# Waiting tasks that sleep, wider pacing, and a sixth pair in seven products, in a GLA + NSA + SwiGLU layer

## The chip, the core and the metric

One core of one Trainium2 chip runs the whole layer in one launch. The metric is the device time of an execution in microseconds; of several executions the median is given. A profiled execution is timed too; its trace covers a span a little shorter than its time.

## What is computed

A decoder layer on 256 tokens of width 2048, all in float32: two attention groups, gated linear attention (GLA, 4 heads) and native sparse attention (NSA, 8 query heads over 2 key heads), read one normalised input through one projection; their outputs go through one output projection; a SwiGLU feed-forward block (FFN) of width 5632 follows.

```python
n = rms_norm(x, attn_norm_g)
g_qkv, g_lr, g_out, nq, kc, vc, ks, vs, kw, vw, ng = split(n @ w_in)
q, k, v = split(silu(causal_short_conv(g_qkv, gla_conv_w)))       # width 4
gla = rms_norm(chunked_gla(q, k, v, log_sigmoid(g_lr @ w2 + b) / 16), norm_g) * silu(g_out)
nsa = g0 * attend(q, compress(kc, vc)) + g1 * attend(q, selected(ks, vs)) + g2 * attend(q, window(kw, vw))
h = x + concat(gla, nsa) @ w_out
m = rms_norm(h, ffn_norm_g)
out = h + (silu(m @ w_gate) * (m @ w_up)) @ w_down
```

## The kernel before

**Split numbers.** Every weight block and activation is split into a rounded part hi (a copy on ScalarE, ACT) and a rest lo (a subtraction on VectorE, DVE): lines 137 and 138 for `w_in` and `w_out`, 641 and 642 in the FFN. A product is then three matmuls (hi x hi, hi x lo, lo x hi). A main matmul is 128x128 by 128x512; there are 2,592 at line 283 (projections and the FFN's down part), 1,896 at line 1147 (gate and up) and 90 at line 1288.

**Main work and side work.** A projection `proj(c0, evac)` of 512 columns is 96 main matmuls and ends in evictions (L478 for the GLA blocks and kc/vc). The projections run in the order: gate and low-rank columns, q, k, v in two blocks, kc/vc, ks/vs, kw/vw, nq in two blocks; then `w_out` in two halves; then the FFN's blocks. What the mixers do between them is written as generators and put into `urgent` or `later`: `conv` (the short convolution, with `turn_pair` for the transposes at L210 and STT steps at L492, then `to_qk` or `to_v` with the Silu at L502 or L510), `gla_decay` (exp at L545 and L547, DVE at L551 to L558, products at L584), `gla_turn`, `compress` (Silu at L794, product at L803), `turn_kc`, `key_turn`, `turn_q`, and `nsa_mix` (L930 and L941 belong to its compressed branch).

`drive(mains, pace)` draws main matmuls; each is worth 2 units, and for every `pace` units it calls `side()` once. `side()` goes on with the first task of `urgent`, or of `later` if there is none. A task that must give other engines time yields: each bare `yield` uses up one call of `side()`, with nothing done, while all tasks behind it stand still. A third queue, `background`, is called once every `rate` units: `sum_rows` loads FFN weights (SP queue), adds them on DVE (L1079) and stores the sums through the POOL queue (L1083).

**What sets the order.** The order in which the program issues work comes from these calls, then from a scheduler and from the pools' buffers (4 hi and 4 lo, 8 PSUM banks). Each engine then works through its own list in order: an instruction at the head that waits holds up all behind it on that engine. On ACT an ACT_TABLE_LOAD stands wherever exp follows Silu or Silu follows exp.

**Pairs in the FFN.** Gate and up of one block of 512 columns take eight pairs of weight blocks. A pair is either plain (24 main matmuls) or done in seven products (21 main matmuls), for which sums of the weight rows are needed: made beforehand by `sum_rows` for the pairs in `SUMS`, or on the spot by DVE (L1178, L1179, L1180). Block 1 has the order 0, 1, 2, 6, 3, 4, 5, 7, the set (0, 2, 3, 4, 5) in seven products, and prepared sums for 2, 3, 4, 5.

Of the kernel before, what the change touches and what calls it, by code (L numbers as in the profile page):

```python
# [17 lines left out]
NT = S // P  # L18
# [19 lines left out]
def kernel(  # L38
# [43 lines left out]

    def side():

        for queue in (urgent, later):
            while queue:
                try:
                    next(queue[0])
                    return
                except StopIteration:  # L90
                    queue.pop(0)
# [123 lines left out]

    cols = kp.tile([P, 164], F32, name="cols")
# [8 lines left out]
    def cols_rest():  # L225
        for _ in range(8):
            yield
        nc.gpsimd.memset(w2b, 0.0)
        with behind(last["dma"]):
            small_loads()  # L230
        for _ in range(20):
            yield
        pc = bank()
        transpose(pc[:, 0:P], rows2)
        transpose(pc[:, P:P + 20], rows[:20, :], 20)
        nc.vector.tensor_copy(cols[:, 36:164], pc[:, 0:P])
        nc.vector.tensor_copy(cols[:, 16:36], pc[:, P:P + 20])
        TS(kgain, gains[:, 1:4], gains[:, 0:1], None, ALU.mult)

# [241 lines left out]
    def conv(u, ct, dst):  # L481

        for _ in range(8):
            yield
        for pair in range(2):
            ps = yield from turn_pair(u, pair)
            y = g2([2, S])
            for c in range(2):
                ch = ct + 2 * pair + c
                act(y[:, c, :], ps[:, c, :], AF.Copy, scale=cw[:, 3, ch:ch + 1])  # L490
                for i in range(1, 4):
                    STT(y[:, c, i:], ps[:, c, :S - i], cw[:, 3 - i, ch:ch + 1], y[:, c, i:], ALU.mult, ALU.add)  # L492
            yield from dst(pair, y)
# [6 lines left out]
    def to_qk(near, far):  # L500
        def f(pair, y):
            act(near[:, pair, 0 if near is kk else 1], y[:, :, 0:P], AF.Silu)  # L502
            act(far[:, pair, 0 if far is qq else 1], y[:, :, S - 1:P - 1:-1], AF.Silu)
            yield
        return f

    def to_v(b):
        def f(pair, y):
# [4 lines left out]
            for _ in range(10):  # L513
                yield
# [12 lines left out]
    GAP0, GAP1 = 8, 4  # L527
# [100 lines left out]
    def gla_turn(h, y):  # L628
        for _ in range(20):
            yield  # L630
        if h % 2 == 0:
            m_h[h // 2], m_l[h // 2] = g4([4, S], F32R), g4([4, S], F32R)
        p = bank()
        for j in range(2):
            for t in range(NT):
                transpose(p[:, j * S + t * P:j * S + (t + 1) * P], y[:, t, j * P:(j + 1) * P])
            yield
        put_mix(h // 2, slice(2 * (h % 2), 2 * (h % 2) + 2), slice(0, S), p.rearrange("p (j s) -> p j s", j=2))

# [7 lines left out]
    def gla_mix():  # L647
        res = [{} for _ in range(4)]
        yield from gla_decay(0, GAP0)
# [28 lines left out]
    def turn_kc(u):  # L678
        for _ in range(8):
            yield  # L680
# [44 lines left out]
    def key_turn(br, t, kk):  # L725
        for _ in range(15):
            yield
# [7 lines left out]
        STT(kl, pv, g, f32(kh), ALU.mult, ALU.subtract)  # L735

# [14 lines left out]
    def compress():  # L751
# [13 lines left out]
        for w in range(2):  # L765
# [21 lines left out]
            for _ in range(6):  # L787
                yield
# [10 lines left out]
            for _ in range(9):  # L799
# [48 lines left out]
    def turn_q(kv, q):  # L848
        for _ in range(18):
            yield  # L850
# [99 lines left out]
    def nsa_mix():  # L950
# [3 lines left out]
        def ready(u):  # L954
            while u[0] not in nq:
# [17 lines left out]
    def w_out_half(half):  # L973
        for n in range(4):
# [21 lines left out]
    PAIRS7, FIRST7 = tuple(range(8)), {0: (0, 2, 4), 1: (0, 2, 3, 4, 5)}  # L996
# [278 lines left out]
    def down_last():  # L1275
# [68 lines left out]
        for t, bk in enumerate((banks[4], at[1])):  # L1344
# [12 lines left out]
    rate[0] = 18  # L1357
    drive([proj(C_KC, ev_kc), proj(C_KS, ev_kv(0)),
           proj(C_KW, ev_kv(1), ((0, 256), (256, 280))), proj(C_NQ, ev_nq(0))], 2.5)
    later.append(nsa_mix())  # L1360
    drive([proj(C_NQ + 512, ev_nq(1))], 2.5)
    rate[0] = 14
    drive([w_out_half(0)], 2)
# [46 lines left out]
```

## Time and profile before

| | us |
|---|---|
| median of 3 runs | 1107.42 (1107.02 to 1109.54) |
| the profiled execution's own time | 1108.26 |
| its span in the trace | 1106.5 |
| PE busy, of the span | 1096.7 |
| DVE busy | 992.7 |
| ACT busy | 751.5 |

The stages lie roughly so in the trace: input projections and mixers to 385 us, the second half of `w_out` to 417 us, FFN block 0 and block 1's gate and up from there to about 500 us, then seven-product blocks alternating with down parts of 96 matmuls to the end. PE rows of a trace are pipelined: a matmul's row is 0.39 us long while the next one starts 0.23 us after it. A note in brackets gives how long an engine sat idle before the row, and what it waited for.

### The profile page before, as it was taken

The numbers are of one execution on the slowest core, as the hardware profiler recorded it, in microseconds if no ns is written. First come the engines' busy times: TensorE is split into PE (matmuls) and PEld (weight loads), VectorE is DVE, ScalarE is ACT, GpSimd is POOL, SyncE is SP. The second block draws the span as 40 slices with busy tenths as digits, with TensorE's granted clock in tenths as the row PEclk, the third lists the DMA queues.
The fourth block names the chain that finished last, engine by engine and source line by source line (L and its number), as shares of the span: only waits on it lengthen the run. The fifth ranks groups of instructions, "written<-read, shape, count | busy, mean of one in ns | idle before, by whom it ended". The sixth has DMA issues, their size and how long they took to land.

```text
span 1106.5 us, 14596 instructions
## 1 busy us (share of the span) xinstructions
PE 1096.7 (99%) x5290; PEld 900.4 (81%) x5290; DVE 992.7 (90%) x1277; ACT 751.5 (68%) x1017; POOL 71.7 (6%) x134
## 2 busy tenths in 40 slices
PE   9999999999999999999999999999999999999998
PEld 8888788897777787888888788888888888888886
DVE  6678887879689788997999999999999999999997
ACT  6646867554566596667586776768586866768684
POOL 4110000123200000000000000000000000000000
PEclk9999999999999999999999999999999999999999
DMA  7999677579765646785565657566665657577763
GB/s 271 340 332 346 210 256 243 196 274 375 282 239 192 236 154 218 242 307 200 192 219 202 217 185 256 195 234 215 216 227 201 214 198 252 182 252 234 237 229 114
DMA packets 124850, 259.61 MB, mean 235 GB/s; under 512 B 6709, under 2 KB 8793, under 8 KB 124778
## 3 DMA queue, kind: packets, MB, share of 16 engines
q1 hardware_dynamic: 113514, 219.86, 58.1%
q0 software_dynamic: 10368, 37.75, 9.2%
q10 hardware_dynamic: 896, 1.07, 0.3%
q8 instruction: 41, 0.67, 0.3%
q14 instruction: 31, 0.25, 0.1%
HBM read 239.78 MB, written 18.87 MB: 234 GB/s over the span
## 4 chain that ended last, share of the span: by engine, by line
PE 88%; DVE 5%; DMA 3%; ACT 3%; issue 1%; POOL 0%; ACTq 0%; DVEq 0%
PE bank L283 44%; PE bank L1147 36%; PE bank L210 3%; DMA raw<-in_w_in_dram 2%; PE bank L1288 2%; DVE ftwo L642 2%; DVE lo L138 1%; PE bank L584 1%; PE bank L946 1%; PE bank L873 1%; ACT hi L137 1%; DMA fraw<-in_w_down_dram 1%; ACT ftwo L641 0%; PE bank L779 0%; DVE g L1178 0%
## 5 line engine op out<-in xcount | busy, mean ns | idle before, releaser
L1147 PE MATMUL bank<-ftwo,g 128*128 128x512 f32 x1848 | 431.6, 392 | 0.2 <-ACT ftwo L641 0.2
L1147 PEld LDWEIGHTS bank<-ftwo,g 128*128 128x128 f32 x1848 | 342.4, 188 | 76.6 <-DVE ftwo L642 3.3
L283 PE MATMUL bank<-hi,g 128*128 128x512 f32 (+1 forms) x1088 | 321.5, 375 | 0.3 <-ACT hi L137 0.2
L642 DVE TENSOR_TENSOR ftwo<-fraw,ftwo 128x1536 fp32r<-128x1536 f32 (+1 forms) x130 | 257.9, 1984 | 8.8 <-ACT ftwo L641 7.5
L641 ACT ACTIVATE ftwo<-fraw 128x1536 fp32r<-128x1536 f32 (+1 forms) x130 | 216.9, 1670 | 32.9 <-DMA fraw<-in_w_up_dram 23.2
L283 PE MATMUL bank<-ftwo,g 128*128 128x512 f32 x960 | 221.4, 391 | 0.4 <-ACT bank L1259 0.4
L283 PEld LDWEIGHTS bank<-hi,g 128*128 128x128 f32 x1088 | 192.4, 188 | 31.7 <-issue 0.8
L283 PEld LDWEIGHTS bank<-ftwo,g 128*128 128x128 f32 x960 | 179.2, 188 | 39.9 <-ACT bank L1259 2.6
L137 ACT ACTIVATE hi<-raw 128x1024 fp32r<-128x1024 f32 (+3 forms) x124 | 130.6, 1057 | 95.8 <-PE bank L283 73.2
L283 PE MATMUL bank<-lo,g 128*128 128x512 f32 (+3 forms) x544 | 193.6, 375 | 0.9 <-DVE lo L138 0.6
L138 DVE TENSOR_TENSOR lo<-raw,hi 128x1024 fp32r<-128x1024 f32 (+3 forms) x124 | 150.0, 1216 | 34.3 <-ACT hi L137 33.6
L641 ACT ACTIVATE ftwo<-g 128x1024 fp32r<-128x1024 f32 x74 | 78.2, 1057 | 69.4 <-DVE g L1178 41.1
L283 PEld LDWEIGHTS bank<-lo,g 128*128 128x128 f32 x544 | 98.4, 188 | 16.1 <-DVE lo L138 1.0
L642 DVE TENSOR_TENSOR ftwo<-g,ftwo 128x1024 fp32r<-128x1024 f32 x74 | 90.3, 1220 | 10.5 <-ACT ftwo L641 10.5
L642 DVE TENSOR_TENSOR ftwo<-fsum,ftwo 128x1024 fp32r<-128x1024 f32 x74 | 90.2, 1219 | 0.0
L641 ACT ACTIVATE ftwo<-fsum 128x1024 fp32r<-128x1024 f32 x74 | 77.5, 1048 | 6.4 <-DVE fsum L1180 5.1
L1271 ACT COPY g<-bank 128x512 f32<-128x512 f32 x80 | 45.9, 589 | 39.4 <-PE bank L283 37.6
L1178 DVE TENSOR_TENSOR g<-fraw 128x1024 f32<-128x1024 f32 x56 | 67.5, 1219 | 0.0
L1259 ACT COPY bank<-g 128x512 f32<-128x512 f32 x80 | 45.2, 593 | 14.3 <-DVE f L1208 13.0
L641 ACT ACTIVATE g<-bank 128x512 fp32r<-128x512 f32 x46 | 27.3, 599 | 33.0 <-PE bank L210 27.4
L210 PE MATMUL bank<-ident,g 128*128 128x128 f32 (+3 forms) x230 | 42.5, 277 | 1.5 <-ACT g L1043 0.7
L1136 POOL DMA_DIRECT2D g<-sums x16 | 8.5, 531 | 511.5 <-DVE ftwo L642 482.8
(247 smaller groups left out, 908.3 us busy)
## 6 DMA issues: line engine op xcount, KB each, us to landing
fraw<-in_w_gate_dram SPq DMA_DIRECT2D x86, 512.0 KB, 4.0
fraw<-in_w_down_dram SPq DMA_DIRECT2D x42, 1024.0 KB, 5.1
raw<-in_w_in_dram SPq DMA_DIRECT2D x36, 1024.0 KB, 6.5
fraw<-in_w_up_dram SPq DMA_DIRECT2D x70, 512.0 KB, 4.8
sums<-g POOLq DMA_DIRECT2D x32, 512.0 KB, 5.0
raw<-in_w_out_dram SPq DMA_DIRECT2D x16, 1024.0 KB, 5.8
g<-in_w_gate_dram SPq DMA_DIRECT2D x16, 512.0 KB, 7.4
g<-in_w_up_dram SPq DMA_DIRECT2D x16, 512.0 KB, 8.1
```

Source lines behind the costliest of these rows:

```text
L137: act(h[:, i:i + n], r[:, k + i:k + i + n], AF.Copy)
L138: last["d"] = TT(o[:, i:i + n], r[:, k + i:k + i + n], f32(h[:, i:i + n]), ALU.subtract)
L210: return nc.tensor.transpose(o, i, ident[:n, :n])
L283: last["mm"] = mm(bk[t], a[:, k, t * P:(t + 1) * P], m[:, off:off + w], start=(first_ and k == 0 and i == 0), stop=(end and k == 3 and i = ...
L584: mm(p[:, j * P:(j + 1) * P], u, w, start=True, stop=True)
L641: act(hi, ps, AF.Copy)
L642: last["d"] = TT(lo, ps, f32(hi), ALU.subtract)
L1147: mm(banks[q], x, m, start=todo[q] == total[q], stop=todo[q] == 1)
L1178: TT(s1, r[:, 1:3], r[:, 3:4].to_broadcast([P, 2, 512]), ALU.add)
L1259: nc.scalar.copy(banks[qs[n][t]], h_sb[n][:, t, :])
L1271: nc.scalar.copy(h_sb[n][:, t, :], bs[t])
L1288: mm(bk, u, m, start=(first and i == 0), stop=(end and i == 2), skip_group_check=onto)
```

## The change

Three things change. Line numbers after it are 7 to 10 higher.

1. **Sleeping tasks.** A task in `urgent` may `yield N`: it then sleeps for N calls of `side()`, and each call goes to the first task that is awake, or to `later` if all sleep. The rows of bare yields in `conv`, `to_v`, `gla_turn`, `turn_kc`, `key_turn` and `turn_q` become one such sleep, with larger numbers. Since tasks may now pass one another, `gla_mix` and `nsa_mix` look into a set `done` before they go on.
2. **Wider pace.** The pace goes from 2.5 to 2.8 (kc to the first nq block), from 2.5 to 2.7 (second nq block) and from 2 to 2.6 (first half of `w_out`); `sum_rows` is called every 16 instead of every 18 units in that part. `compress` waits 10 and 14 calls instead of 6 and 9, the GLA's second gap is 6 instead of 4.
3. **A sixth pair.** Pair 1 of FFN block 1 is done in seven products. No sums are prepared for it.

```diff
+    asleep = {}
     def side():
+        for task in urgent:
+            asleep[task] = max(asleep.get(task, 0) - 1, 0)
         for queue in (urgent, later):
-            while queue:
+            while True:
+                task = next((t for t in (urgent if queue is urgent else later[:1]) if not asleep.get(t)), None)
+                if task is None:
+                    break
                 try:
-                    next(queue[0])
+                    asleep[task] = next(task) or 0
                     return
                 except StopIteration:
-                    queue.pop(0)
+                    queue.remove(task)
...
     def conv(u, ct, dst):
-        for _ in range(8):
-            yield
+        yield 14
...
     def to_v(b):
-            for _ in range(10):
-                yield
+            yield 16
...
-    GAP0, GAP1 = 8, 4
+    GAP0, GAP1 = 8, 6
...
     def gla_turn(h, y):
-        for _ in range(20):
-            yield
+        yield 22
...
     def gla_mix():
+        while not all((i, pair) in done for i in (False, True) for pair in range(2)):
+            yield
...
     def turn_kc(u):
-        for _ in range(8):
-            yield
+        yield 12
...
     def key_turn(br, t, kk):
-        for _ in range(15):
-            yield
+        yield 18
...
-            for _ in range(6):
+            for _ in range(10):
                 yield
             pt = bank()
...
-            for _ in range(9):
+            for _ in range(14):
                 yield
             pk = bank()
...
     def turn_q(kv, q):
-        for _ in range(18):
-            yield
+        yield 20
...
         def ready(u):
-            while u[0] not in nq:
+            while u[0] not in nq or not all(("key", br, t) in done for br in range(2) for t in range(NT)):
                 yield
...
-    PAIRS7, FIRST7 = tuple(range(8)), {0: (0, 2, 4), 1: (0, 2, 3, 4, 5)}
+    PAIRS7, FIRST7 = tuple(range(8)), {0: (0, 2, 4), 1: (0, 1, 2, 3, 4, 5)}
...
-    rate[0] = 18
+    rate[0] = 16
     drive([proj(C_KC, ev_kc), proj(C_KS, ev_kv(0)),
-           proj(C_KW, ev_kv(1), ((0, 256), (256, 280))), proj(C_NQ, ev_nq(0))], 2.5)
+           proj(C_KW, ev_kv(1), ((0, 256), (256, 280))), proj(C_NQ, ev_nq(0))], 2.8)
     later.append(nsa_mix())
-    drive([proj(C_NQ + 512, ev_nq(1))], 2.5)
+    drive([proj(C_NQ + 512, ev_nq(1))], 2.7)
     rate[0] = 14
-    drive([w_out_half(0)], 2)
+    drive([w_out_half(0)], 2.6)
```

The instructions move at many places. Three of them follow, as they stand in each engine's list (numbers behind a name tell buffers apart).

The first place is the start of the ks projection, on ACT and PE. In the order before, ACT has there one eviction of a kc/vc bank (L478), the Silu of the last v block (L510, L511), and the table load of the next decays:

```order
L137 ACTIVATE hi_302_1886<-raw_301_1884 128x2x512
L478 ACTIVATE g4_285_1816<-bank_247_1583,rx_122 128x512
L510 ACTIVATE g2_265_1678<-g2_264_1669 128x2x128
L511 ACTIVATE g2_265_1678<-g2_264_1669 128x2x128
L545 ACT_TABLE_LOAD
L545 ACTIVATE g2_272_1721<-g4_80_566 128x64x4
```

The order after has two such evictions, a hi, and a table load in front of the Silu (lines are 9 or 10 higher: L487, L144, L520):

```order
L499 ACTIVATE g2_272_1725<-bank_271_1717,cols_116 128x256
L487 ACTIVATE g4_290_1831<-bank_248_1590,rx_122 128x512
L487 ACTIVATE g4_290_1831<-bank_249_1591,rx_122 128x512
L144 ACTIVATE hi_315_1938<-raw_312_1932 128x2x512
L520 ACT_TABLE_LOAD
L520 ACTIVATE g2_273_1734<-g2_272_1725 128x2x128
L521 ACTIVATE g2_273_1734<-g2_272_1725 128x2x128
L554 ACT_TABLE_LOAD
L554 ACTIVATE g2_274_1739<-g4_80_566 128x8x32
```

The Silu has moved behind the second eviction, whose bank (249) takes the last matmul of its projection, and a table load now stands directly in front of it. On PE the transposes that read the Silu's output stood before with the first matmul of the ks projection between them:

```order
L283 MATMUL bank_248_1584<-lo_282_1771,g4_55_361 128x512
L283 MATMUL bank_248_1584<-hi_281_1770,g4_56_362 128x512
L210 MATMUL bank_266_1694<-ident_109,g2_265_1678 128x128 x2
L283 MATMUL bank_286_1819<-hi_289_1823,g4_24_147 128x512
L210 MATMUL bank_266_1694<-ident_109,g2_265_1678 128x128 x2
L283 MATMUL bank_286_1819<-lo_290_1824,g4_24_147 128x512
```

and after, all four stand in front of that projection's first matmul (L292, bank_291), with four decay products (L593) behind them:

```order
L292 MATMUL bank_249_1591<-lo_283_1778,g4_55_361 128x512
L292 MATMUL bank_249_1591<-hi_282_1777,g4_56_362 128x512
L217 MATMUL bank_284_1784<-ident_109,g2_273_1734 128x128 x4
L593 MATMUL bank_289_1821<-g4_17_134,g4_16_133 128x128
L593 MATMUL bank_289_1821<-g4_16_133,g4_17_134 128x128
L593 MATMUL bank_289_1821<-g2_234_1500 128x128
L593 MATMUL bank_289_1821<-g2_245_1554 128x128
L292 MATMUL bank_291_1834<-hi_294_1838,g4_24_147 128x512
L292 MATMUL bank_291_1834<-lo_295_1839,g4_24_147 128x512
```

The main matmuls of the ks projection have moved behind four transposes and four decay products.

The second place is the GLA's first decays, on ACT, during the k and v projections. Before, the Silu of q or k (L502, L503) and the decays' exp (L545, L547) alternate:

```order
L502 ACT_TABLE_LOAD
L502 ACTIVATE g4_16_133<-g2_173_1116 128x256
L503 ACTIVATE g4_17_134<-g2_173_1116 128x256
L545 ACT_TABLE_LOAD
L545 ACTIVATE g2_183_1204<-g4_80_566 128x64x4
L502 ACT_TABLE_LOAD
L502 ACTIVATE g4_16_133<-g2_175_1135 128x256
L503 ACTIVATE g4_17_134<-g2_175_1135 128x256
L547 ACT_TABLE_LOAD
L547 ACTIVATE g2_183_1204<-g4_81_567 128x64x4
L137 ACTIVATE hi_191_1256<-raw_190_1254 128x2x512
L547 ACTIVATE g2_189_1237<-g4_81_567 128x32x8
```

After, the two Silu groups (L511, L512) stand together, and the hi (L144) that stood behind the last of these loads has another place:

```order
L144 ACTIVATE hi_191_1252<-raw_190_1250 128x2x512
L511 ACT_TABLE_LOAD
L511 ACTIVATE g4_16_133<-g2_173_1122 128x256
L512 ACTIVATE g4_17_134<-g2_173_1122 128x256
L511 ACTIVATE g4_16_133<-g2_175_1142 128x256
L512 ACTIVATE g4_17_134<-g2_175_1142 128x256
L554 ACT_TABLE_LOAD
L554 ACTIVATE g2_188_1220<-g4_80_566 128x64x4
L556 ACTIVATE g2_188_1220<-g4_81_567 128x64x4
L144 ACTIVATE hi_193_1256<-raw_190_1250 128x2x512
L556 ACTIVATE g2_189_1244<-g4_81_567 128x32x8
L144 ACTIVATE hi_200_1303<-raw_199_1301 128x2x512
```

One Silu group has moved up beside the other, and one pair of table loads between them is gone. The compression's Silu (L794, after it L804) moves in the same manner, to 34 main matmuls ahead of its product (L803, after it L813).

The third place is DVE in FFN block 1, from the end of pair 0 (its last lo reads `fsum_841`) through pair 1 (`fraw_845`) to pair 2 (`fraw_850` before). Before, pair 1 is one lo of 2048:

```order
L642 TENSOR_TENSOR ftwo_846_4660<-fraw_845_4657,ftwo_846_4660 128x2048
L1224 SCALAR_TENSOR_TENSOR f2_828_4533<-f2_830_4535,rf_142,f2_828_4533 128x512
L1223 TENSOR_TENSOR f2_832_4537<-bank_801_4334,f2_832_4537 128x512
L642 TENSOR_TENSOR ftwo_842_4636<-fsum_841_4623,ftwo_842_4636 128x1024
L1224 SCALAR_TENSOR_TENSOR f2_831_4536<-f2_832_4537,rf_142,f2_831_4536 128x512
L1029 TENSOR_TENSOR f2_847_4675<-g4_784_4273,g4_785_4274 128x512
L642 TENSOR_TENSOR ftwo_851_4700<-fraw_850_4697,ftwo_851_4700 128x1536
```

and after, a lo of 1536, three sums and two lo of 1024:

```order
L651 TENSOR_TENSOR ftwo_846_4660<-fraw_845_4657,ftwo_846_4660 128x1536
L1234 SCALAR_TENSOR_TENSOR f2_828_4533<-f2_830_4535,rf_142,f2_828_4533 128x512
L1233 TENSOR_TENSOR f2_832_4537<-bank_801_4334,f2_832_4537 128x512
L651 TENSOR_TENSOR ftwo_842_4636<-fsum_841_4623,ftwo_842_4636 128x1024
L1234 SCALAR_TENSOR_TENSOR f2_831_4536<-f2_832_4537,rf_142,f2_831_4536 128x512
L1188 TENSOR_TENSOR g4_847_4663<-fraw_845_4657 128x1024
L1189 TENSOR_TENSOR fsum_848_4664<-g4_847_4663,fraw_845_4657 128x512
L1190 TENSOR_TENSOR fsum_848_4664<-fsum_848_4664,fraw_845_4657 128x512
L651 TENSOR_TENSOR ftwo_849_4677<-g4_847_4663,ftwo_849_4677 128x1024
L651 TENSOR_TENSOR ftwo_854_4707<-fraw_853_4704,ftwo_854_4707 128x1536
L651 TENSOR_TENSOR ftwo_849_4677<-fsum_848_4664,ftwo_849_4677 128x1024
```

The lo of pair 2 (`fraw_850` before, `fraw_853` after) has moved behind pair 1's three sums and one of its two lo parts.

More of the change, by code (lines that the diff above doesn't have):

```diff
@@ L213, in rsqrt_ @@
         nc.gpsimd.tensor_tensor(o, i, mhalf[:i.shape[0], :i.shape[1]], ALU.pow)
+    done = set()
     cols = kp.tile([P, 164], F32, name="cols")
@@ L238, in cols_rest @@
         TS(kgain, gains[:, 1:4], gains[:, 0:1], None, ALU.mult)
+        done.add("cols")
     def flip(src, q, gcol, hi, lo, pairs=range(2), between=None):
@@ L481, in conv @@
     def conv(u, ct, dst):
-        for _ in range(8):
-            yield
+        assert "cols" in done
+        yield 14
         for pair in range(2):
@@ L503, in f @@
             act(far[:, pair, 0 if far is qq else 1], y[:, :, S - 1:P - 1:-1], AF.Silu)
+            done.add((near is kk, pair))
             yield
@@ L638, in gla_turn @@
         put_mix(h // 2, slice(2 * (h % 2), 2 * (h % 2) + 2), slice(0, S), p.rearrange("p (j s) -> p j s", j=2))
+        done.add(("out", h))
     def in_parts(hi, lo, ps):
@@ L735, in key_turn @@
         STT(kl, pv, g, f32(kh), ALU.mult, ALU.subtract)
+        done.add(("key", br, t))
     kcm = cp.tile([P, 2 * NCMP], F32, name="kcm")
@@ L973, in w_out_half @@
     def w_out_half(half):
+        assert all(("out", h) in done for h in range(4))
         for n in range(4):
```

## The prediction, made before the result was known

> **What bounds the kernel now.** I read the page's engine and clock lines first, then the chain of waits, then busy time by windows, and last the instructions around each stop of TensorE (PE). One granted clock and one busy engine:
>
> ```profile
> PE 1096.7 (99%) x5290; PEld 900.4 (81%) x5290; DVE 992.7 (90%) x1277; ACT 751.5 (68%) x1017; POOL 71.7 (6%) x134
> PEclk9999999999999999999999999999999999999999
> PE 88%; DVE 5%; DMA 3%; ACT 3%; issue 1%; POOL 0%; ACTq 0%; DVEq 0%
> 655.35 32.85 PE bank L1147 x144
> ```
>
> PE works 99% of the span, and the chain that ended last lies on it for 88%. The last row, of that chain, gives the price of a matmul: 32.85 us for 144, or **0.228 us** from start to start. So time can only go in two ways: fewer matmuls, or fewer stops. The windows (busy us of PE, PEld, DVE, ACT, POOL with counts, then clock, DMA share, GB/s) say where the stops are:
>
> ```profile
> 80.00:280.00 200.00, 197.12 (x1085) 165.20 (x1084) 166.83 (x326) 126.20 (x229) 27.19 (x37) 1.00 0.79 275
> 280.00:385.00 105.00, 104.27 (x579) 82.91 (x578) 86.95 (x196) 60.67 (x142) 9.22 (x13) 1.00 0.65 230
> 450.00:470.00 20.00, 20.00 (x90) 16.57 (x89) 19.78 (x26) 12.18 (x11) 0.53 (x1) 1.00 0.68 220
> 500.00:530.00 30.00, 30.00 (x137) 24.57 (x136) 24.09 (x25) 20.43 (x27) 0.00 (x0) 1.00 0.50 169
> ```
>
> In the mixers, 80 to 385 us, PE idles 2.88 + 0.73 = 3.6 us. A record is 0.39 us long where the next starts 0.23 us later, so each stop hides 0.16 us more; I find about a dozen, so the stops cost some **5.5 us**. That is the most the new calling order can win. The largest, PE's and ACT's rows in time (start, length, engine, line):
>
> ```profile
> 82.50 0.33 PE L210 MATMUL bank<-ident,g 128*128 128x128 f32 x1
> 83.08 0.33 PE L210 MATMUL bank<-ident,g 128*128 128x128 f32 x1 [0.24 <-ACT g L478]
> ...
> 121.19 0.39 PE L283 MATMUL bank<-hi,g 128*128 128x512 f32 x1
> 121.81 0.73 PE L283 MATMUL bank<-hi,g 128*128 128x512 f32 x2 [0.23 <-ACT hi L137]
> 123.12 0.50 PE L283 MATMUL bank<-lo,g 128*128 128x512 f32 x1 [0.58 <-DVE lo L138]
> ...
> 276.06 0.39 PE L283 MATMUL bank<-hi,g 128*128 128x512 f32 x1
> 277.74 0.40 PE L803 MATMUL bank<-cw,g 128*30 128x128 f32 x2 [1.29 <-ACT g L794]
> 276.16 1.28 ACT L794 ACT_TABLE_LOAD   x1
> 277.45 0.23 ACT L794 ACTIVATE g<-g 128x32 f32<-128x32 f32 x1
> ...
> 180.33 0.39 PE L283 MATMUL bank<-hi,g 128*128 128x512 f32 x1
> 181.12 0.44 PE L210 MATMUL bank<-ident,g 128*128 128x128 f32 x2 [0.41 <-ACT g L510]
> ```
>
> Starts beyond their 0.23 us: (0.62 - 0.23) + (1.31 - 0.46) = 1.2, with a late start behind it 1.3 us at 121 us; 1.68 - 0.23 = 1.45 at 276; 0.79 - 0.23 = 0.56 at 180. The rest of the 5.5 is split over small stops, the largest about 0.5 us at 82 us (0.58 between two transposes).
>
> **What the change removes.** (a) Stops. In the new order the table load and Silu of the compression (L794) stand 34 main matmuls, 7.7 us, ahead of the product that reads it, against 1.68 us between its two neighbours now; the chain at 121 us has one table load less and its lo parts 14 matmuls ahead; the transposes of 82 us come later than their conv. I take all of the 5.5 us as gone, and 4 as the other end, since a chain of equal length with other neighbours can catch a matmul again. (b) Three main matmuls of the sixth pair: 3 x 0.228 = **0.7 us**. (c) Some matmuls run slower behind a plain-fp32 product:
>
> ```profile
> 150.66 0.48 PE L283 MATMUL bank<-hi,g 128*128 128x512 f32 x1
> 150.97 0.40 PE L283 MATMUL bank<-lo,g 128*128 128x512 f32 x1
> ```
>
> 0.31 us to the next start, 0.09 more than 0.23. The new order has seven such passages fewer: **0.6 us**; with none of it, zero.
>
> **What it adds.** (d) The new order puts a table load on the path where the last block of v is turned, at the start of the ks projection (the 0.56 us stop of 180 us). ACT now and the row of its load:
>
> ```profile
> 178.08 1.06 ACT L137 ACTIVATE hi<-raw 128x1024 fp32r<-128x1024 f32 x1 [1.35 <-issue]
> ...
> 179.65 0.62 PE L283 MATMUL bank<-hi,g 128*128 128x512 f32 x2
> 180.07 0.69 ACT L478 ACTIVATE g<-bank,rx 128x512 f32<-128x512 f32 x1 [0.93 <-PE bank L283]
> 180.66 0.41 ACT L510 ACTIVATE g<-g 128x256 f32<-128x256 f32 x1
> 181.39 1.28 ACT L545 ACT_TABLE_LOAD   x1
> ```
>
> Now ACT evicts a kc/vc bank (L478) when three matmuls of that projection are left, has the Silu table loaded, and goes straight to L510. After, both evictions come first, and the second needs the projection's very last matmul; behind it stand a hi of 1.06, the load of 1.28 (the decays' exp has taken the Silu table away) and L510. From the last matmul's start: 0.42 to the eviction (now it starts at 180.07 for a matmul that starts at 179.65), 0.60 until the next ACT step can start (180.07 to 180.66), 1.05, 1.28, 0.41: 3.75 us until the transposes, which stand next on PE. Less 0.23: **3.5 us**, from 2.8 (if the second eviction costs nothing) to 3.9 (if DVE's last conv step ends later). Queued behind the transposes are four decay products and the whole ks projection, though its hi and lo are ready; DVE and ACT run ahead meanwhile, so nothing shortly after is late. (e) At the first matmul of w_out half 0 PE has a product of the compressed branch (L941) right behind DVE's last step:
>
> ```profile
> L930 DVE TENSOR_TENSOR g<-bank,g 15x512 fp32r<-15x512 f32 x4 | 2.7, 683 | 0.2
> L893 DVE TENSOR_REDUCE sm<-sm 128x4 f32<-128x60 f32 x4 | 0.8, 209 | 0.8 <-ACT sm L891 0.8
> L901 DVE RECIPROCAL sm<-sm 128x8 f32<-128x8 f32 x4 | 0.8, 194 | 0.0
> ```
>
> 0.68 for L930 behind six short steps of about 0.2 that stand in front of it, less what runs while PE is still at the preceding matmul: **1.1 us**, or nothing if DVE is that much ahead. (f) The first v block has a load in front of its Silu too, five matmuls (1.1 us) ahead: 0.4; DVE has some 47 steps in a bunch before a lo used two matmuls later: 0.3, up to 0.8; four places of 0.1 to 0.2: 0.5. Together **1.2**, from 0 to 2. (g) Pair 1 of block 1 in seven products, whose row sums nobody prepared: DVE makes them.
>
> ```profile
> L1178 DVE TENSOR_TENSOR g<-fraw 128x1024 f32<-128x1024 f32 x56 | 67.5, 1219 | 0.0
> L1179 DVE TENSOR_TENSOR fsum<-g,fraw 128x512 f32<-128x512 f32 x56 | 38.4, 687 | 0.7
> L1180 DVE TENSOR_TENSOR fsum<-fsum,fraw 128x512 f32<-128x512 f32 x56 | 38.5, 688 | 0.9
> L642 DVE TENSOR_TENSOR ftwo<-g,ftwo 128x1024 fp32r<-128x1024 f32 x74 | 90.3, 1220 | 10.5 <-ACT ftwo L641 10.5
> 459.97 2.28 DVE L642 TENSOR_TENSOR ftwo<-fraw,ftwo 128x2048 fp32r<-128x2048 f32 x1
> 463.43 1.21 DVE L642 TENSOR_TENSOR ftwo<-fsum,ftwo 128x1024 fp32r<-128x1024 f32 x1
> 465.83 1.75 DVE L642 TENSOR_TENSOR ftwo<-fraw,ftwo 128x1536 fp32r<-128x1536 f32 x1
> 463.24 4.02 PE L1147 MATMUL bank<-ftwo,g 128*128 128x512 f32 x17
> ```
>
> DVE gains 1.22 + 0.69 + 0.69 + 2 x 1.22 and a lo of 1.75 for 2.28: **+4.5 us**, there where it is busy 19.78 of 20 us. The plain pair 1 was what let DVE catch up: 2.28 us of DVE for 24 matmuls, 5.5 us. At pair 0's end (463.43 + 1.21 = 464.64) its last lo is only some 0.4 us early for the matmuls that read it. So about 0.55 us are missing inside pair 1 and 0.95 at the next wide lo: **1.5 us**, then DVE's 5.9 idle us of 500 to 530 take up the rest. Nothing is lost if DVE's evictions slip behind instead; all 4.5 if no later idle time can be used. ACT gains two conversions of about 1 us and is at 12.18 of 20 us: hidden. (h) The row sums prepared every 16 instead of 18 units move SP loads, DVE's L1079 and POOL's issues earlier by a ninth; PE waits for none of them now. Free; if DVE's room were gone, 0.68 each.
>
> **Sum.** -5.5 - 0.7 - 0.6 + 3.5 + 1.1 + 1.2 + 1.5 = **+0.5 us**, against the profiled execution's 1108.26 us (span 1106.5, 1.76 around it), so 1108.8. That execution stands 0.84 above the median of the runs, 1107.42, so I forecast **1107.9**.
>
> One price is disputed. The row of 276.16 shows a table load of 1.28 us and the Silu starting as it ends; the profile has no further pause there. The Trainium skill, page "ScalarE: Activation LUTs", section "What ACT_TABLE_LOAD costs", adds a drain of 1.38 us to each switch. By that (d) would be 4.9 us and the time an estimated 1109.3; this trace disagrees.
>
> **Rivals.** (1) *Covered*: faster. The long wait (d) comes, as its chain is all on ACT and in order, but DVE is ahead by more than I gave it, so (e), (f) and (g) all but vanish: 3.5 + 0.3 - 6.8 = -3.0, **1104.4 us**. For it: PE's stop at (d) hands DVE 3.5 us, and DVE is at 166.83 of 200 us in the mixers. Against it: 19.78 of 20 us in the block. (2) *DVE sets the pace from block 1 on*: slower. Pair 1 takes 4.5 us of DVE; if the idle time of 500 to 530 us is there only because its next inputs are not, PE pays 3.0 more than the 1.5, **1110.9 us**. It decides from the point where DVE's lead at pair 0's end is under the 0.4 us of now. Against it: those windows show PE never waiting at 500 to 530 though DVE idles. (3) *A long stop lowers the clock*: slower. PE's longest stop in the mixers is the 1.45 us at 276, behind which the clock stays 1.00; (d) would be longer than any stop that the trace shows. Should the granted clock halve behind it for as long as the stop itself, 3.5 / 0.456 = 7.7 matmuls cost 0.228 more each, 1.75 us: **1109.7 us**. The Trainium skill, page "TensorE: Matmul & The Clock Gate", section "Why this matters for your kernels", warns of idle gaps over some 3 us, after which the clock drops to half; no run here shows it, since no gap is that long.
>
> **How the numbers follow.** The forecast has 0.49, its own range 1105.3 to 1109.6; covered 0.28; DVE 0.14; clock 0.09. A measurement of this kernel tells about 0.2%, 2.2 us, from no change: faster means under 1105.2, slower over 1109.6. So faster 0.28, same 0.49, slower 0.14 + 0.09 = 0.23. The bounds together would reach from 2.8 - 6.8 = -4.0 (1103.4) to 3.9 + 1.1 + 2 + 4.5 - 4 - 0.7 = +6.8 (1114.2); leaving out the tails, 1103.8 to 1111.0.
>
> **What would show it.** Right: no PE wait over 0.3 us for L794's Silu (now at another line number) or at the q and k conv; a PE gap of 3 to 4 us before four transposes at about 180 us, ended by L510's Silu behind a table load; about 1 us before the first w_out matmuls; two gaps under 1 us, for DVE's lo, at 455 to 475 us. Wrong: no gap at 180 us, which makes it faster by 3.5 us than forecast; matmul starts 0.4 us apart behind it, or PE waiting for DVE at 600 us and later, which makes it slower.

## The result and the profile after

The change makes the kernel **slower**: a median of 1118.89 us (1118.24 to 1120.03, 4 runs) against 1108.48 us before (1107.02 to 1109.73, 4 runs), a ratio of 1.0096, 95% interval 1.0077 to 1.0114. That lies above the predicted range. The profiled execution took 1120.03 us, with a span of 1118.2 us, 11.7 us more than the span before.

First the page of the changed kernel: span, engines, and the chain that ended last by engine.

```profile
span 1118.2 us, 14595 instructions
PE 1098.7 (98%) x5287; PEld 900.8 (81%) x5287; DVE 998.2 (89%) x1282; ACT 757.6 (68%) x1023; POOL 70.9 (6%) x134
PE 79%; issue 8%; DVE 5%; DMA 4%; ACT 2%; POOL 1%; ACTq 0%; SPq 0%; POOLq 0%; DVEq 0%
```

PE does three matmuls fewer and is busy 2.0 us longer, so 9.7 of the 11.7 us are idle time. The same stretches as in the prediction, in the changed kernel (busy us of PE, PEld, DVE, ACT, POOL, then clock, DMA share, GB/s), and FFN block 0's, which the prediction looked at in part:

```profile
80.00:280.00 200.00, 193.45 (x1118) 163.49 (x1117) 164.76 (x327) 126.52 (x228) 27.07 (x38) 0.99 0.77 269
280.00:385.00 105.00, 103.98 (x525) 82.72 (x525) 86.84 (x192) 61.89 (x139) 7.99 (x11) 1.00 0.65 232
420.00:470.00 50.00, 47.31 (x204) 36.77 (x203) 41.12 (x46) 30.70 (x35) 2.80 (x5) 1.00 0.56 201
500.00:530.00 30.00, 29.64 (x134) 23.84 (x133) 27.87 (x27) 22.72 (x27) 0.00 (x0) 1.00 0.64 224
```

The stretch of FFN block 0 in the kernel before, for comparison:

```profile
420.00:470.00 50.00, 49.76 (x221) 40.37 (x220) 44.89 (x48) 33.22 (x34) 3.33 (x6) 1.00 0.77 252
```

PE's idle time in 80 to 280 us goes from 2.88 to 6.55 us, and 2.7 us stand in FFN block 0, where PE hardly waited (0.24) and where the prediction has no term at all. The starts of main matmuls of the same number, counted from the program's start, say where the time is lost:

| place | before, us | after, us | difference | added in this part |
|---|---|---|---|---|
| first gate and up matmul (the mixers and w_out are done) | 416.91 | 422.48 | 5.6 | 5.6 |
| main matmul 1748, behind block 0's two stops | 445.10 | 454.36 | 9.3 | 3.7 |
| main matmul 2012, behind block 1's gate and up | 505.94 | 517.97 | 12.0 | 2.8 |
| to the end, and three matmuls fewer | | | 11.7 | 0.4 - 0.7 |

Three losses, then, and the waits of PE name them (engine, line waited for: us in total, times, longest):

```profile
PE bank L217 <- ACT g L520: 3.7, 2, 3.5
PE bank L1157 <- DVE ftwo L651: 2.2, 2, 1.2
PE bank L1157 <- ACT ftwo L650: 1.6, 4, 0.6
PE bank L217 <- DVE g L796: 1.4, 1, 1.4
PE bank L789 <- DVE g L784: 1.0, 1, 1.0
PE bank L882 <- DVE g L651: 0.7, 1, 0.7
PE bank L813 <- ACT g L804: 0.5, 1, 0.5
```

The wait for the compression's Silu, 1.29 us before, is down to 0.5 at an earlier place; those at the q and k conv are gone. The first row is the stop that was forecast, (d). The four rows from L796 to L813 are stops in the mixers that were not forecast. **The first loss, the mixers**, in time: PE's rows on both sides of the long stop, ACT's chain, and DVE's last conv step.

```profile
177.92 0.39 PE L292 MATMUL bank<-hi,g 128*128 128x512 f32 x1
181.76 0.75 PE L217 MATMUL bank<-ident,g 128*128 128x128 f32 x4 [3.45 <-ACT g L520]
...
177.67 1.37 ACT L487 ACTIVATE g<-bank,rx 128x512 f32<-128x512 f32 x2 [0.62 <-PE bank L292]
178.93 1.05 ACT L144 ACTIVATE hi<-raw 128x1024 fp32r<-128x1024 f32 x1
180.00 1.28 ACT L520 ACT_TABLE_LOAD   x1
181.29 0.42 ACT L520 ACTIVATE g<-g 128x256 f32<-128x256 f32 x1
...
179.31 0.47 DVE L501 SCALAR_TENSOR_TENSOR g<-bank,cols,g 128x253 f32<-128x253 f32 x1
```

From 177.92 to 181.76 is 3.84 us, 3.61 beyond a matmul's 0.23, and each link of the chain is there with the length that (d) gave it. DVE ends its last conv step (L501) at 179.78, so ACT, not DVE, is the last link. The next two windows are the first matmuls behind the stop:

```profile
182.00:184.00 2.00, 2.00 (x13) 1.94 (x12) 0.27 (x2) 1.97 (x5) 0.00 (x0) 0.62 0.81 248
184.00:186.00 2.00, 2.00 (x8) 1.67 (x8) 2.00 (x7) 1.49 (x6) 0.00 (x0) 0.53 0.98 348
```

The granted clock falls to 0.62 and 0.53 for four microseconds. Then PE meets late work at 215, 229 and 236 us. The chain of the last two, on DVE, ACT and PE:

```profile
229.05 0.28 DVE L796 COPY g<-bank 128x128 f32<-128x128 f32 x1
232.32 0.69 DVE L1089 TENSOR_TENSOR g<-g 128x512 f32<-128x512 f32 x1 [2.98 <-DMA g<-in_w_up_dram]
...
234.11 0.28 DVE L802 TENSOR_REDUCE g<-bank 128x32 f32<-128x128 f32 x1
...
234.47 1.28 ACT L804 ACT_TABLE_LOAD   x1 [5.33 <-DVE g L802]
...
236.05 0.40 PE L813 MATMUL bank<-cw,g 128*30 128x128 f32 x2 [0.48 <-ACT g L804]
```

A row sum (L1089), which nobody on PE waits for, stands at the head of DVE's list for 2.98 us until its weights arrive. Behind it stands L802, whose result ACT needs for the Silu, whose result PE needs. That is how the "free" step (h) cost something, though not in every execution: in e2 below, with the same order here, L1089 waited 2.40 us and PE did not stop at L813.

**The second loss, FFN block 0.** The issue of the gate weights' second load on the SP queue, after, and the DVE row that ends just before it:

```profile
430.62 0.37 SPq L1116 DMA_DIRECT2D fraw<-in_w_gate_dram  x1
...
429.82 0.69 DVE L651 TENSOR_TENSOR g<-g,g 128x512 fp32r<-128x512 f32 x1 [0.34 <-ACT g L650]
```

The same load in the kernel before:

```profile
419.01 0.37 SPq L1106 DMA_DIRECT2D fraw<-in_w_gate_dram  x1
```

Before, 2.1 us behind the first gate and up matmul; after, 8.1 us behind it. What comes of it, on ACT, DVE and PE:

```profile
442.92 1.49 ACT L650 ACTIVATE ftwo<-fraw 128x1536 fp32r<-128x1536 f32 x1 [4.41 <-DMA fraw<-in_w_up_dram]
...
444.44 1.76 DVE L651 TENSOR_TENSOR ftwo<-fraw,ftwo 128x1536 fp32r<-128x1536 f32 x1 [3.42 <-ACT ftwo L650]
...
449.98 1.64 PE L1157 MATMUL bank<-ftwo,g 128*128 128x512 f32 x6 [0.91 <-DVE ftwo L651]
452.86 7.33 PE L1157 MATMUL bank<-ftwo,g 128*128 128x512 f32 x31 [1.25 <-DVE ftwo L651]
```

The cause is a placement. This FFN buffer takes memory that the mixers' buffers have given back (bytes 132864 to 141056 of a partition, by the built program). The tile that holds the last quarter's second turned pair of h, read by L651, lay at byte 163008 before, and lies at 138432 after, as buffers are freed in another order. So the load must now wait for that tile's last reader, which ends at 429.82 + 0.69 = 430.51, where before its last wait was for an ACT step of 418.2 us. The SP queue's own list of waits has both, after and before:

```profile
SPq L1116 <- DVE g L651: 21.1, 1, 21.1
```

```profile
SPq L1106 <- ACT g L264: 15.0, 1, 15.0
```

**The third loss, FFN block 1:** two stops of 0.7 us each at 476.85 and 485.89, where pair 1 needs more of DVE, and one of 0.55 at 515.7. Before, the matmul ahead of that last stop started at 504.35 us, when DVE was still busy throughout; the idle 5.9 us of DVE in 500 to 530 us began at 508.8. (The whole run is some 10 us later now, so the two windows of 500 to 530 us do not hold the same work.)

### The profile page after: what moved, and what is told of

It reads as the page before. It is cut to its first block, busy times and chain, and to the rows that moved or that the text cites. A ratio compares the mean times of both kernels' runs of the same rounds, so it can differ in the third digit from the quotient of the medians.

```text
span 1118.2 us, 14595 instructions
## 1 busy us (share of the span) xinstructions
PE 1098.7 (98%) x5287; PEld 900.8 (81%) x5287; DVE 998.2 (89%) x1282; ACT 757.6 (68%) x1023; POOL 70.9 (6%) x134
## 4 chain that ended last, share of the span: by engine, by line
PE 79%; issue 8%; DVE 5%; DMA 4%; ACT 2%; POOL 1%; ACTq 0%; SPq 0%; POOLq 0%; DVEq 0%
PE bank L292 42%; PE bank L1157 30%; DVE ftwo L651 2%; PE bank L217 2%; PE bank L1298 2%; DMA fraw<-in_w_up_dram 1%; DMA g<-in_w_up_dram 1%; PE bank L955 1%; DMA sums<-g 1%; PE bank L593 1%; DMA fraw<-in_w_down_dram 1%; DVE g L1188 1%; PE bank L882 1%; DVE lo L145 0%; ACT ftwo L650 0%
## 5 line engine op out<-in xcount | busy, mean ns | idle before, releaser
L292 PE MATMUL bank<-hi,g 128*128 128x512 f32 (+1 forms) x1088 | 323.7, 376 | 1.3 <-ACT hi L332 1.3
L651 DVE TENSOR_TENSOR ftwo<-fraw,ftwo 128x1536 fp32r<-128x1536 f32 (+1 forms) x130 | 257.4, 1982 | 9.2 <-ACT ftwo L650 8.0
L292 PE MATMUL bank<-ftwo,g 128*128 128x512 f32 x960 | 221.8, 391 | 1.0 <-ACT bank L1269 0.6
L292 PEld LDWEIGHTS bank<-hi,g 128*128 128x128 f32 x1088 | 191.8, 189 | 30.7 <-ACT hi L332 1.7
L292 PEld LDWEIGHTS bank<-ftwo,g 128*128 128x128 f32 x960 | 179.2, 188 | 41.0 <-ACT bank L1269 2.9
L144 ACT ACTIVATE hi<-raw 128x1024 fp32r<-128x1024 f32 (+3 forms) x124 | 130.6, 1057 | 98.1 <-PE bank L292 75.1
L292 PE MATMUL bank<-lo,g 128*128 128x512 f32 (+3 forms) x544 | 193.1, 374 | 0.0
L292 PEld LDWEIGHTS bank<-lo,g 128*128 128x128 f32 x544 | 98.5, 189 | 15.1 <-DVE lo L145 0.4
L651 DVE TENSOR_TENSOR ftwo<-g,ftwo 128x1024 fp32r<-128x1024 f32 x75 | 91.6, 1221 | 9.4 <-ACT ftwo L650 9.3
L651 DVE TENSOR_TENSOR ftwo<-fsum,ftwo 128x1024 fp32r<-128x1024 f32 x75 | 91.5, 1220 | 0.0
L217 PEld LDWEIGHTS bank<-ident,g 128*128 128x128 f32 (+3 forms) x230 | 30.8, 142 | 17.7 <-ACT g L520 4.5
```

The source lines that it names most:

```text
L144: act(h[:, i:i + n], r[:, k + i:k + i + n], AF.Copy)
L217: return nc.tensor.transpose(o, i, ident[:n, :n])
L292: last["mm"] = mm(bk[t], a[:, k, t * P:(t + 1) * P], m[:, off:off + w], start=(first_ and k == 0 and i == 0), stop=(end and k == 3 and i = ...
L651: last["d"] = TT(lo, ps, f32(hi), ALU.subtract)
```

## The experiments

Ratios are to runs of the kernel before on the same chip; its medians there were 1107.76 (e1 to e4), 1107.81 (e5 to e8) and 1107.80 us (e9 to e12).

### The sixth pair alone, and all but the sixth pair

The first is the kernel before with the new table, the second the changed kernel with the old one:

```diff
-    PAIRS7, FIRST7 = tuple(range(8)), {0: (0, 2, 4), 1: (0, 2, 3, 4, 5)}
+    PAIRS7, FIRST7 = tuple(range(8)), {0: (0, 2, 4), 1: (0, 1, 2, 3, 4, 5)}
```

> The kernel before with the sixth pair alone, calling order and pace as before. Theory A (the pair costs DVE about 2 us net in block 1 and no more; the other FFN loss has another cause): PE stops for DVE's lo within pair 1 and at the next wide lo, 1.4 us, plus some 0.5 to 1 us until the down part, less 0.7 for three matmuls: 1109 to 1111 us, +1 to +2 on the kernel before. Rival B (all 6 us that the FFN lost come from the pair, because DVE sets the pace there): 1113 to 1115 us.

Measured: 1109.9 us (10 runs), ratio 1.0022 [1.0013, 1.0032]: the pair costs **2.1 us**, as theory A has it, by stops in block 1 of 0.70, 0.62 and 0.19 us and one of 0.55 at the start of the down part, with no stop in block 0 that the kernel before doesn't have.

> The changed kernel without the sixth pair. Theory A: the stops in block 0 (3.2 us between 445 and 453 us of the changed kernel's trace) stay, only about 2 us go: 1116.5 to 1117.5 us. Rival B: the FFN's whole loss of 6 us goes: 1112.5 to 1113.5 us.

Measured: 1116.84 us (4 runs), ratio 1.0086 [1.0069, 1.0103], 2.05 below the changed kernel, the same price from the other side. The two large stops of block 0 stay, at 1.2 and 1.4 us, so they belong to the calling order. In this execution the long stop did not lower the clock. Its window there:

```profile
182.00:184.00 2.00, 2.00 (x16) 1.88 (x15) 0.52 (x2) 1.99 (x5) 0.00 (x0) 1.00 0.83 233
```

PE's row in time 6 us behind the stop:

```profile
187.40 0.49 PE L593 MATMUL bank<-g 128*128 128x128 f32 x2 [0.70 <-DVE g L576]
```

At full clock PE ran into DVE's decays (L576) instead and gained only 0.28 us on the changed kernel over this place. The lowered clock cost little here, since PE would have waited.

### Another buffer for the last turned pair

```diff
-            v = g2([2, S])
+            v = (g4 if n == 3 and pair else g2)([2, S])
```

> The changed kernel with one buffer moved: the last quarter's second turned pair of h is held in a g4 buffer, not in a g2 buffer. Theory A: in the changed kernel that g2 buffer happens to lie where the FFN's second raw weight block goes, so that block's load waits for the last conversion of h (430.6 us, before 419.0) and starves ACT and DVE; with the buffer elsewhere the load is issued some 11 us earlier and the 3.2 us of stops in block 0 go: 1115 to 1116 us. Rival B: the late load costs nothing that DVE would not lose anyway: 1118 to 1119 us.

Measured: 1116.45 us (4 runs), ratio 1.0078 [1.0063, 1.0093], 2.4 less than the changed kernel; that lies 0.45 above theory A's range and 1.5 below rival B's. The load on the SP queue in this kernel:

```profile
413.06 0.37 SPq L1116 DMA_DIRECT2D fraw<-in_w_gate_dram  x1
```

And the window of block 0:

```profile
420.00:470.00 50.00, 49.54 (x220) 40.08 (x219) 44.37 (x49) 30.90 (x35) 2.80 (x5) 1.00 0.52 179
```

One tile in another pool, and the load leaves 17.6 us earlier, PE's idle time there falls from 2.69 to 0.46 us, and both stops are gone. In all kernels of this study in which such a tile lies at byte 138432 (the changed one, e2, e5, e7, e12) block 0 lost 2.9 to 3.7 us; in those in which it doesn't (e1, e3, e6, e8 to e11) it lost nothing.

### What a stop does to the clock

This kernel leaves the whole layer out and stores x. PE runs 33 bursts of 60 matmuls; between two bursts it waits for a chain of one wide ACT copy and a number of narrow ones (the loop over `narrow` is cut below); each of eleven lengths comes three times.

```python
for i in range(60):
    mm(ps, src[:, 0:P], w0, start=(i == 0), stop=(i == 59))
a = ps
for j in range(wide):
    b = cpy.tile([P, 512], F32R, tag="c", name=f"c_{n}_{j}")
    act(b, a, AF.Copy, scale=0.01)
    a = b
...
src = a
```

> A kernel of its own that computes nothing of the layer (it stores x): 33 bursts of 60 matmuls 128x512, each followed by a stop of about 1 to 6 us, three times each length, made by a chain of ACT copies that the next burst reads. Theory A (a long stop alone lowers the granted clock): behind stops of up to about 2 us the matmuls go on 0.23 us apart; behind stops of 3.5 us and more, some or all bursts begin 0.43 us apart for 3 to 4 us. Rival C (the slow matmuls at 182 to 186 us in the changed kernel come from the mix of fp32 products there, not from the stop): 0.23 us apart behind every stop.

Measured (673.63 us, one run): PE's rows in time, one burst behind each of the shorter stops, and both kinds behind the third:

```profile
26.32 13.89 PE L62 MATMUL bank<-w,c 128*128 128x512 f32 x60 [0.69 <-ACT c L66]
...
71.42 15.52 PE L62 MATMUL bank<-w,d 128*128 128x512 f32 x60 [2.05 <-ACT d L70]
...
125.45 13.89 PE L62 MATMUL bank<-w,d 128*128 128x512 f32 x60 [3.42 <-ACT d L70]
142.76 15.53 PE L62 MATMUL bank<-w,d 128*128 128x512 f32 x60 [3.41 <-ACT d L70]
```

The clock (behind ACT's and POOL's busy time here, as DVE does nothing) in a window with stops of 0.69 us, and in one right behind a stop of 2.05:

```profile
24.00:41.00 17.00, 15.63 (x69) 12.30 (x67) 1.19 (x2) 0.00 (x0) 1.00 0.00 1
89.00:92.60 3.60, 3.60 (x10) 2.80 (x11) 0.00 (x0) 0.00 (x0) 0.57 0.00 0
```

Idle for 0.69 us: 13.89 us, three times of three. Idle for 2.05 us: 15.5 us, three of three, with matmuls 0.43 us apart at a clock of 0.57 first. For 3.42 us: twice longer, once not. For 3.75 and more (23 bursts): always, by 1.4 to 2.9 us. So rival (3)'s mechanism is real, its size of 1.75 us was near, and it needs less than a stop of 3.5 us; rival C is out. That the same stop may or may not draw it fits the changed kernel (clock lowered) and e2 (not).

### The transposes behind other work

The last v block's turn sleeps 40 calls instead of 16, and its transposes are issued behind the latest main matmul:

```diff
-            yield 16
+            yield 40 if b and pair else 16
...
+                    with behind(last["mm"]) if b and pair else nullcontext():
                         transpose(p[:, t * S + c * P:t * S + (c + 1) * P], v[:, c, t * P:(t + 1) * P])
```

> The changed kernel with the four transposes of the last v block held back by some 37 matmuls (the task sleeps 40 calls instead of 16 there, and the transposes stand behind the main matmul last issued). Theory A (the 3.6 us stop at 178 us and the half clock behind it are lost time of their own): the stop and the slow matmuls go, 3.6 to 5 us less: 1114 to 1115.3 us. Rival D (the chain behind it, decays on ACT and DVE, is what is late; PE only waits at the first place that needs it): the stop goes, but the clock's part brings nothing and some of the wait returns within the ks projection, at the transposes or the decay products: 1116 to 1117.5 us.

Measured: 1116.97 us (1114.52 to 1120.56, 4 runs), ratio 1.0087 [1.007, 1.0104]. The stop (d) is gone and the profiled execution, 1114.52, lost only 0.3 us up to w_out's second half; but the runs spread over 6 us, and the median, in rival D's range, is only 1.9 below the changed kernel. The mean granted clock goes with the spread: 1.000 in the run of 1114.52, 0.998 in those of 1116.79 and 1117.16, 0.997 in that of 1120.56. The test was repeated below without the other two losses.

### The sleeping alone, and the old pace

The first is the changed kernel with all its old numbers and five pairs: only the new way of waiting is left.

```diff
-        yield 14
+        yield 8
...
-            yield 16
+            yield 10
...
-    GAP0, GAP1 = 8, 6
+    GAP0, GAP1 = 8, 4
...
-    rate[0] = 16
+    rate[0] = 18
```

(and so on for the other waits, the paces of 2.8, 2.7 and 2.6, and the pair.)

> The changed kernel with only the sleeping: all waits, paces and the rate of the row sums as before, five pairs as before. Theory E (sleeping itself bunches the work: the calls that waiting tasks used to burn now go to the decays, DVE gets them in one lump and what follows is late): the mixers end, by the first matmul of w_out's second half, 3 to 6 us later than in the kernel before (371.1 us there, 376.5 in the changed kernel), with PE stops at the end of the kc projection and in the ks and kw projections; 1111 to 1114 us. Rival F (the wider waits and paces make the stops): the mixers end within 1 us of the kernel before, 1107 to 1108.5 us.

Measured: 1128.61 us (4 runs), ratio 1.0189 [1.0175, 1.0203]. That is far above both ranges: theory E's stops came, but the mixers end 20.5 us later, not 3 to 6. PE's waits in it:

```profile
PE bank L217 <- ACT g L520: 8.4, 2, 5.0
PE bank L616 <- DVE g L588: 2.0, 1, 2.0
```

The second has the changed kernel's paces and rate set back:

```diff
-    rate[0] = 16
+    rate[0] = 18
...
-           proj(C_KW, ev_kv(1), ((0, 256), (256, 280))), proj(C_NQ, ev_nq(0))], 2.8)
+           proj(C_KW, ev_kv(1), ((0, 256), (256, 280))), proj(C_NQ, ev_nq(0))], 2.5)
```

(and 2.7 to 2.5, 2.6 to 2.)

> The changed kernel with the old paces (2.5, 2.5, 2) and the old rate of 18, its sleeps, wider waits and sixth pair kept. Theory E: stops in the same places, the mixers end 4 to 6 us later than in the kernel before, 1117 to 1119.5 us. Rival F: the mixers end within 2 us of the kernel before, 1113 to 1115 us.

Measured: 1119.12 us (4 runs), ratio 1.0103 [1.0089, 1.0117], in theory E's range. The long stop is the same; of the four behind it that of 236 us is gone and the others are 0.58, 1.43 and 1.35 us. Up to w_out's second half e6, with the old numbers, loses 20.5 us, the changed kernel 5.4 and e7 5.4. So the loss of the mixers comes from the sleeping itself; the longer sleeps and waits repair about three quarters of what it breaks, and the pace moves small stops but changes nothing in the sum.

### The calling order alone, and the transposes again

The changed kernel with five pairs and e3's buffer, then the same with e5's edit on top. The first against the changed kernel:

```diff
-    PAIRS7, FIRST7 = tuple(range(8)), {0: (0, 2, 4), 1: (0, 1, 2, 3, 4, 5)}
+    PAIRS7, FIRST7 = tuple(range(8)), {0: (0, 2, 4), 1: (0, 2, 3, 4, 5)}
...
-            v = g2([2, S])
+            v = (g4 if n == 3 and pair else g2)([2, S])
```

> The changed kernel without the sixth pair and with the last turned pair of h in a g4 buffer: of the change there remain the sleeping, the wider waits and the pace. Theory A (three costs that add up: mixers 5.4 us, buffer 3.7, pair 2.1 to 2.8): the FFN takes as long as in the kernel before, only the mixers' 5.4 us remain, 1112.5 to 1113.5 us. If the FFN parts had a common cause, less or more than their sum would go: over 1114 or under 1112.

Measured: 1113.28 us (5 runs), ratio 1.0058 [1.0045, 1.0071], as expected: **5.5 us** for the calling order, with its waits and pace. With 2.1 for the pair and 2.4 to 3.6 for the buffer (with the pair, after against e3; without, e2 against e9) that makes 10.0 to 11.2; measured are 10.4.

> The same with the four transposes of the last v block held back as before. Theory A (the stop of 3.6 us and what follows it are lost time of their own): about 5 us less than the kernel without that, 1107.5 to 1109 us, and no slow clock at 180 us. Rival D (PE would wait for the same chain a little later in most executions): 1110 to 1112 us.

Measured: 1109.74 us (11 runs), ratio 1.0014 [1.0005, 1.0023]: 3.5 less than e9, between the two ranges. Three of the other stops stay, with one grown from 1.5 to 2.0 (that of 236 us is not there):

```profile
PE bank L217 <- DVE g L797: 2.0, 1, 2.0
PE bank L790 <- DVE g L785: 0.9, 1, 0.9
PE bank L883 <- DVE g L652: 0.7, 1, 0.7
```

(L797, L785 and L652 are the changed kernel's L796, L784 and L651.) So these are no consequence of the long stop; they have their own cause in the order of the side work.

That 3.5 is close to the stop's own 3.61 is chance: two effects offset each other. Of the 11 runs, four had a mean clock of 1.000 and took 1108.37 to 1109.27 us; the other seven, at 0.998 or 0.999, took 1109.54 to 1110.41. The profiled execution is one of the seven. It and e5's both have the grown stop (2.02 and 2.03 us idle, up to 224.8 us); the window right behind it, in e10 and in e5:

```profile
225.00:228.50 3.50, 3.50 (x19) 3.50 (x19) 2.02 (x4) 1.95 (x3) 0.00 (x0) 0.53 0.85 326
225.00:228.50 3.50, 3.50 (x31) 3.50 (x31) 1.84 (x4) 2.24 (x4) 0.00 (x0) 1.00 0.86 331
```

With the clock at 0.53, e10 falls 1.5 us behind e5 here and does not win it back before the FFN. So where the clock was kept, holding the transposes back brought 4.9 us (the median of the four, 1108.42, against e9's 1113.28, whose runs all had a mean clock of 0.997 or 0.998), about what theory A said; in most runs the next stop then lowered the clock and took some 1.4 of it back.

### Who gets the calls of the sleepers

In the changed kernel a call for which all urgent tasks sleep goes to `later`, where the decays stand. Here `later` gets every second such call, and in the other kernel none:

```diff
                 if task is None:
                     break
+                if queue is later and urgent:
+                    turn[0] += 1
+                    if turn[0] % 2:
+                        return
```

> The changed kernel in which the second queue (decays and the rest of the mixers) gets only every second call while tasks of the first sleep. Theory E (the calls freed by sleeping go to the decays in one lump, and DVE's lump makes the v block and the compression late): the lump at 150 to 161 us is thinner, the stop at the end of the kc projection is under 2 us or gone, and the mixers end 2 to 5 us earlier than the changed kernel's 376.5. Rival G (the lump is not the cause, the wider conv wait alone makes the last v block late): the stop stays within 0.5 us of 3.6.

Measured: 1117.47 us (4 runs), ratio 1.0089 [1.0075, 1.0103]. Its waits (lines are 4 higher than in the changed kernel):

```profile
PE bank L221 <- ACT g L524: 3.5, 1, 3.5
PE bank L221 <- DVE g L736: 3.0, 1, 3.0
```

The small stops (L784, L796, L882, L950 of the changed kernel) are gone, by the distances between PE's starts; the long one stays as it was, and a new one of 3.0 us stands at a later turn. Theory E's forecast failed here: the stop was to shrink, and the mixers end 1.2 us later than in the changed kernel, not 2 to 5 earlier.

> The same, but the second queue gets no call at all while a task of the first sleeps, as in the kernel before. Theory E: no stop over 1 us at the end of the kc projection; but with the wider pace the decays and the attention may come so late that a tail of mixer work stands behind w_out's first half, so the total may be anywhere from 1108 to 1125 us. Rival G: the stop stays within 0.5 us of 3.6.

Measured: 1132.1 us (4 runs), ratio 1.0223 [1.0209, 1.0237]. Here the stop at the ks projection is back at its old 0.57 us, with no table load in front of the Silu. This is theory E's sign, and rival G, which had the stop stay in both kernels, is out; the time lies above the range that E gave. The work kept back lies behind w_out's first half as a tail in which PE waits:

```profile
PE bank L954 <- DVE g L943: 4.2, 2, 2.1
PE bank L793 <- DVE bank L781: 3.4, 1, 3.4
```

So the calls that sleepers set free bring the decays' exp in front of the last Silu and with it the table load. Giving away half of them is already enough for that; giving away none costs more than it saves.

### The one wait that paid, in the old kernel

The largest old stop was the compression's Silu, 1.45 us at 276 us. The kernel before with nothing but a longer wait there:

```diff
-            for _ in range(9):
+            for _ in range(16):
                 yield
             pk = bank()
```

> The kernel before with one number changed: compress waits 16 calls instead of 9 between its Silu and the product that reads it, so that 15 matmuls instead of 7 stand between them. Theory A (that stop of 1.45 us, 2.4 in the run with the pair alone, is lost time of its own): it goes and no other takes its place, 1105 to 1106.5 us. Rival: the wait returns later in the attention's first products, 1107 to 1108 us.

Measured: a median of 1106.44 us (11 runs: ten from 1105.40 to 1107.43, and one of 2862.06), ratio of the ten 0.9988 [0.9979, 0.9997], in theory A's range, with the wait for L794 gone. It is the only kernel here that is faster than the kernel before, by 0.1%, less than the 0.2% the prediction counted as faster; the interval just leaves 1 out.

## Why the prediction was wrong

The forecast was +0.5 us against the profiled execution; it became +11.7. By the steps:

- **(a)** The stops that it named are gone, as was said why, but for that of 180 us, in whose place (d) stands. But it took the whole 5.5 us. By the distances between starts the old stops that went are worth 3.9 (0.47 at 82 us, 1.14 at 121, 0.29 at 140.6, which it did not name, 0.57 at 180 and 1.45 at 276). Of the other 1.6, 0.9 was a misreading: the whole 0.73 us of idle time in 280 to 385 us is one stop, at 384.65 before transposes of h, which the change does not touch and which stands at 390.08 after, with the same 0.73. The rest comes from counting "about a dozen" stops where the idle time lies in seven. The 4 given as the other end was the right value.
- **(b)** holds: three matmuls, 0.7 us. **(c)**, 0.6 us, was not measured alone.
- **(d)** holds to 0.1: 3.61 us against 3.5, by the chain that was written down. The drain of 1.38 us that the Trainium skill (page "ScalarE: Activation LUTs", section "What ACT_TABLE_LOAD costs") adds to a switch isn't there: the load of 180.00 lasts 1.28 us and the Silu starts at 181.29.
- **The step that failed first** is the sentence behind (d), "DVE and ACT run ahead meanwhile, so nothing shortly after is late". Stops of 1.14, 1.61, 0.65 and 0.90 us follow at 215, 229, 236 and 318 us, 4.3 together. e10 shows that all but that of 236 us stand there without the long stop too. What was read was the order on PE around stops of the old trace; what was not read is what DVE has in front of each step that a mixer's matmul needs in the new order.
- **(e)** 0.45 for 1.1, **(f)** 0.37 and 0.15 at its two named places for 0.4 and 0.3: right or too dear.
- **(g)** is right in kind and place, mis-sized: 2.8 us against 1.5. The stops in block 1 are 0.69 and 0.74 as forecast together, but a third of 0.55 follows at 515.7, PE loses another 0.2 to 0.3 us in small steps around each of the three, and the third lies ahead of the DVE idle time that was to take up the rest. Behind it that idle time did so: DVE's wait of 2.23 us before the lo of 520.22 is 0.41 after (531.57), and PE loses only 0.4 us more to the end. With (b), e1 measured 2.1 net.
- **(h)** "free" was wrong for a reason other than DVE's room: the moved step waits for a transfer at the head of DVE's list (2.98 us), and the stop of 0.65 at 236 us follows from it. The stop is absent with the old rate and pace (e7), but in e2 too, so it hangs on when that transfer lands.
- **Missing altogether: block 0, 3.7 us.** No step asked where the mixers' tiles lie in memory. The diff doesn't mention it and no row of the trace before could have priced it; the list of waits of each load, before and after, would have shown it, as the load's last wait changes from an ACT step to L651.

The mixers' +5.6 against a forecast of -0.3 are thus 4.3 (unforeseen stops) + 1.6 (a) + 0.3 (clock) - 0.65 (e), 5.55 of 5.9; (c) and what (f) was too dear by are not in this sum. Then 3.7, 1.3 (g) and 0.4 follow behind the mixers.

Of the rivals, *covered* failed with the sentence on DVE, and *DVE sets the pace* didn't come: the idle time was drawn on, and behind main matmul 2012 only 0.4 us are added. *The clock* came, but cost 0.3 us rather than 1.75, because the matmuls that it slowed would have waited for DVE (e2); behind the stop of 2.0 us in e10, where they would not, it cost 1.5. The Trainium skill (page "TensorE: Matmul & The Clock Gate", section "Why this matters for your kernels") puts the gap at over some 3 us; in e4 2.05 us were enough, three times of three, and in e10 2.02 us.

Open stays which sleeping task delays each of the stops at 215, 229 and 318 us: e6 and e11 show that they come and go with the calls, not which call makes which. Why the clock falls behind a stop in one execution and not in another (after and e2, e10 and e5) was not tried, nor whether that alone makes e5's runs spread over 6 us.

## What to carry to other kernels

A waiting list that stands still also keeps order: letting other tasks pass fills the wait, but what passes (here an exp in front of a Silu, a row sum in front of a reduction) decides the next stop, so read in the new order what stands ahead of each step that the busy engine waits for, not only around the old stops. When buffers are released and their memory is used again, a new order of frees can tie a load to a reader that has nothing to do with it; compare what each load waits for, before and after. When one stop is taken out, look at the clock behind the next one: it can take part of the gain. Where a single wait costs the time, lengthen that one: one number (e8) gave more than the whole rewrite.

## What the runs showed of the hardware

- In e4 PE idling for 2.05 us lowered the granted clock each of three times (0.57 in the window shown), idling for 0.69 us never, for 3.42 us in two of three cases; a burst of 60 matmuls then took 1.3 to 2.9 us more. In the layer, 2.02 us lowered it in e10's profiled execution and 2.03 us at the same place in e5's did not.
- What a lowered clock costs depends on the work behind the stop: 0.3 us where that work is late anyway (after against e2), 1.5 us where PE could have gone on (e10 against e5).
